# A hybrid decoder step on one core: one-hot rows of the gate table by matrix products and ACT, and the trunk's GpSimd work moved to DVE and ACT

## The chip, the core and the metric

The kernel runs on one core of one Trainium2 chip. A core has a matrix engine (PE, with its weight loads shown apart as PEld), a vector engine (DVE), a scalar engine (ACT), GpSimd (POOL) and SyncE (SP), which here issues nearly all DMAs. Each engine takes its instructions in order. The metric is device time in microseconds of one execution, all DMAs included.

## The reference

One layer is computed for 1024 prompt tokens and 64 sample tokens, D = 1024, in float32 accuracy. The change touches the following parts; the rest (conv and gated recurrence, caches) stays as it is.

```python
z = _rmsnorm(x) @ w_in              # lru_x | lru_gate | q | k | v | gates
p = softmax(scores, sink)           # sliding window attention, 16 heads
hres = x + merged @ w_out
# PEER: per token 8 heads pick 16 of 128*128 experts
qr = (xn @ w_query); s = einsum('nhpd,hpkd->nhpk', qr, sub_keys)
s_top, i_top = lax.top_k(s, 16)
cand_idx = i_top[0] * 128 + i_top[1]        # 16 x 16 pairs of a head
best, pos = lax.top_k(cand, 16)
idx = take_along_axis(cand_idx, pos)        # 128 experts of a token
g = softmax(best)                           # their weights
act = gelu(x . expert_u[idx]) * g ; y = hres + act @ expert_v[idx]
```

## The kernel before

The tokens are worked off in three blocks (block 0: 256 prompt and 64 sample tokens, blocks 1 and 2: 384 prompt tokens each). For each block the *trunk* runs: query, key and value products, attention, the gate and attention branch (L291), the recurrence `lru`, its gate branch (L307), `w_out` (L326), the second norm (`norm_T`, L239 transposes), and `retrieve`, the 16 products with `peer_w_query` and the top 16 of each half (L732 to L739). Every product is done in three passes in fp32r: a weight tile of 128x1024 is loaded (`wraw`), ACT rounds it to `whi` (L148), POOL computes the remainder `wlo` (L149), and `mm3` (L168 to L170) sums hi*hi, hi*lo and lo*hi. Three buffers each of `wraw`, `whi` and `wlo` let weights run ahead.

While the trunk of block 1 runs, the *background* of block 0 is dealt out in small steps by `bg` between trunk steps, and while that of block 2 runs, the background of block 1. It has two parts. `choose` finds a head's 16 best of 50 candidates and fetches their expert numbers by a comparison (L786, DVE), a multiply (L788, POOL) and a sum (L789, DVE). `build_g` then makes the gate table, for each token a 128x128 matrix with the softmax weights at (expert // 128, expert % 128), as the product of two one-hot matrices. It takes tokens by four, a *group*: 176 groups for the 704 tokens of blocks 0 and 1, 8 groups to a *chunk*. A group is two comparisons and two multiplies on DVE and one multiply on POOL of 128x512 bf16 (the weight comes in three bf16 parts), 12 bf16 matmuls into one PSUM tile and one ACT copy into `sg` (L899); a full `sg` (2 MB, one buffer) is stored in `g_d` (L901).

Then `dense` (from 1915 us) multiplies all 128 tiles of 128 experts with those 704 tokens, weighted by the gate table; the 384 tokens of block 2 gather their experts row by row on POOL's queue instead. In that phase the low parts of weights are POOL's too (`ul`, `vl`).

The order on each engine is written out by a scheduler that plays the program through a model of the engines before it runs: instructions are placed when that model has their inputs ready, and PSUM and SBUF buffers of one tag are handed out in the order of the program text. Transposes, the query scores and the gate table share the tag `tr` with three PSUM tiles. The DMAs stand on SP's queue in the order so found, and one that waits holds up those behind it.

Of the kernel before, what the change touches and what calls it, by code (L numbers as in the profile page):

```python
# [63 lines left out]


# [4 lines left out]
class Kern:  # L70
    def __init__(self, ctx, tc, i, o):
        self.ctx, self.tc, self.nc, self.i, self.o = ctx, tc, tc.nc, i, o
        nc = self.nc
# [112 lines left out]
    def load_c(self, src, c0):  # L186

        nc, sp = self.nc, self.sp
        hi = sp.tile([P, KD, P], F32R, tag="whi", name="whi", bufs=NW)
        lo = sp.tile([P, KD, P], F32R, tag="wlo", name="wlo", bufs=NW)  # L190
        raw = sp.tile([P, KD, P], F32, tag="wraw", name="wraw", bufs=NR)
        nc.sync.dma_start(raw, src.rearrange("(k p) c -> p k c", p=P)[:, :, c0:c0 + P])
        self.split(hi, lo, raw, nc.gpsimd)
        return hi, lo

    def load_n(self, src, c0):
# [3 lines left out]
        for h in range(2):  # L200
# [4 lines left out]
            self.split(hi, lo, raw, nc.gpsimd)  # L205
# [161 lines left out]
    def attention(self, bi, xh, xl, ah, al, raw, bg):  # L367
# [46 lines left out]
        def scores(t, j, qT):  # L414
# [28 lines left out]
            nc.gpsimd.tensor_tensor(sb[:, :, 0:S], sb[:, :, 0:S], z4.unsqueeze(2).to_broadcast([P, 4, S]), op=ALU.mult)  # L443
# [378 lines left out]
    def slots_T(self, ft, r, n0):  # L822

        nc = self.nc
        pt = self.tr((P, 3, P))
        for x in range(3):
            nc.tensor.transpose(pt[:, x, 0:r], ft[0:r, x], self.ident[0:r, 0:r])
        sl = self.xp.tile([P, 3, P], F32, tag="sl", name="sl", bufs=1)
        nc.scalar.copy(sl[:, :, 0:r], pt[:, :, 0:r])
        nc.sync.dma_start(self.sT_d[:, :, n0:n0 + r], sl[:, :, 0:r])  # L830
# [39 lines left out]
    def build_g(self, bi):  # L870

        nc, sp = self.nc, self.sp
        p0, p1, smp, nP, n, tiles = self.geom(bi)
        for ch in range(ROW0[bi] // CH, (ROW0[bi] + n) // CH):
            sg = sp.tile([P, AT], F32, tag="at", name="sg", bufs=1)[:, 0:P * CH].rearrange("p (i n) -> p i n", i=P)
            sT = sp.tile([P, 3, CH], F32, tag="sT", name="sT", bufs=1)
            nc.sync.dma_start(sT, self.sT_d[:, :, ch * CH:(ch + 1) * CH])

            s16 = sp.tile([P, 5, CH], BF16, tag="s16", name="s16", bufs=1)
            nc.scalar.copy(s16[:, 0:3], sT)  # L880
            for x in (2, 3):
                nc.vector.tensor_tensor(sT[:, 2], sT[:, 2], s16[:, x], op=ALU.subtract)
                nc.vector.tensor_copy(s16[:, x + 1], sT[:, 2])
            for t4 in range(CH // 4):
                n0 = t4 * 4
                col = lambda x: s16[:, x, n0:n0 + 4].unsqueeze(1).to_broadcast([P, P, 4])
                oij = self.sp.tile([P, 4, P, 4], BF16, tag=self.otag, name="oij", bufs=N4 if self.otag == "s4" else 6)
                oj, wh, wm, wl = (oij[:, x] for x in range(4))
# [4 lines left out]
                nc.vector.tensor_tensor(wh, wh, col(2), op=ALU.mult)
                pt = self.tr()
                for x in range(4):
                    nc.tensor.matmul(pt[:, x, :], oj[:, :, x], wh[:, :, x], start=True, stop=False)
                    nc.tensor.matmul(pt[:, x, :], oj[:, :, x], wm[:, :, x], start=False, stop=False)
                    nc.tensor.matmul(pt[:, x, :], oj[:, :, x], wl[:, :, x], start=False, stop=True)
                nc.scalar.copy(sg[:, :, t4 * 4:t4 * 4 + 4], pt.rearrange("p x i -> p i x"))  # L899
                if t4 == CH // 4 - 1:  # L900
                    nc.sync.dma_start(self.g_d[ch], sg)  # L901
                yield

# [197 lines left out]
```

## Time and profile before

| | us |
|---|---|
| median of 3 runs | 4001.42 (3998.14 to 4010.92) |
| profiled execution, its own time | 3999.96 |
| its span | 3998.0 |
| PE busy / PEld / DVE / ACT / POOL | 3641.4 / 3477.6 / 3151.0 / 1290.8 / 2407.2 |
| block 0 | about 0 to 525 |
| block 1 with the background of block 0 | about 525 to 1245 |
| block 2 with the background of block 1 | about 1245 to 1915 |
| dense phase | 1915 to 3998 |

Busy time counts an engine as busy while at least one of its instructions runs; a PE instruction's end is modelled, so its busy share is read beside others of the same kind rather than as a distance from the peak. In a row of groups, the mean is that of one instruction from its start to its end; where instructions of an engine overlap a little, their starts stand closer than the mean. "Idle before" is the time in which the engine had nothing to run, with what ended it.

### The profile page before, as it was taken

The numbers are of one execution on the slowest core, as the hardware profiler recorded it, in microseconds if no ns is written. First come the engines' busy times: TensorE is split into PE (matmuls) and PEld (weight loads), VectorE is DVE, ScalarE is ACT, GpSimd is POOL, SyncE is SP. The second block draws the span as 40 slices with busy tenths as digits, with TensorE's granted clock in tenths as the row PEclk, the third lists the DMA queues.
The fourth block names the chain that finished last, engine by engine and source line by source line (L and its number), as shares of the span: only waits on it lengthen the run. The fifth ranks groups of instructions, "written<-read, shape, count | busy, mean of one in ns | idle before, by whom it ended". The sixth has DMA issues, their size and how long they took to land. (4 is left out here: it accounts for less than half of the span.)

```text
span 3998.0 us, 60600 instructions
## 1 busy us (share of the span) xinstructions
PE 3641.4 (91%) x22734; PEld 3477.6 (87%) x22734; DVE 3151.0 (79%) x6798; ACT 1290.8 (32%) x2346; POOL 2407.2 (60%) x1560
## 2 busy tenths in 40 slices
PE   7988998778897878998899999999999999999998
PEld 6778978668895777888799999999999999999998
DVE  6365787999899988998987777777777777777773
ACT  4454353443333435333222222222222222222221
POOL 3444546565554664764576677767766767676651
PEclk8989999889997988999899999999999999999999
DMA  5334523234441133444359898999989899899972
GB/s 148 100 111 149 154 72 90 79 101 145 171 139 56 58 94 108 138 173 162 125 204 308 292 318 303 321 323 316 322 295 311 306 319 316 309 317 310 319 259 80
DMA packets 505654, 821.75 MB, mean 206 GB/s; under 512 B 34220, under 2 KB 360812, under 8 KB 502000
## 3 DMA queue, kind: packets, MB, share of 16 engines
q1 hardware_dynamic: 394768, 415.18, 32.5%
q0 software_dynamic: 110592, 402.70, 28.2%
q8 instruction: 178, 2.92, 0.3%
q14 instruction: 116, 0.95, 0.1%
HBM read 753.25 MB, written 66.50 MB: 205 GB/s over the span
## 5 line engine op out<-in xcount | busy, mean ns | idle before, releaser
L149 POOL TENSOR_TENSOR wlo<-wraw,whi 128x1024 fp32r<-128x1024 f32 x252 | 639.3, 2544 | 513.7 <-ACT whi L148 476.0
L168 PE MATMUL ou<-ah,vh 128*128 128x352 f32 x2048 | 663.4, 327 | 40.6 <-ACT ah L148 23.3
L168 PE MATMUL sc<-dx,uh 128*128 128x352 f32 x2048 | 664.6, 325 | 16.2 <-ACT uh L148 9.0
L169 PE MATMUL ou<-al,vh 128*128 128x352 f32 x2048 | 660.1, 325 | 5.3 <-DVE al L149 5.0
L170 PE MATMUL sc<-dx,ul 128*128 128x352 f32 x2048 | 662.0, 323 | 1.0 <-POOL ul L149 1.0
L169 PE MATMUL sc<-dx,uh 128*128 128x352 f32 x2048 | 662.5, 324 | 0.0
L170 PE MATMUL ou<-ah,vl 128*128 128x352 f32 x2048 | 659.0, 324 | 0.0
L859 DVE SCALAR_TENSOR_TENSOR acc<-row,hv,acc 128x1024 f32<-128x1024 f32 x384 | 493.1, 1284 | 157.3 <-DMA row<-in_expert_v,iA 151.6
L847 DVE SCALAR_TENSOR_TENSOR row<-row,xt 128x1024 f32<-128x1024 f32 x384 | 465.5, 1217 | 174.3 <-DMA row<-in_expert_u,iA 165.0
L857 POOL DMA_INDIRECT row<-in_expert_v,iA x384 | 362.2, 943 | 267.8 <-DVE acc L859 192.6
L845 POOL DMA_INDIRECT row<-in_expert_u,iA x384 | 362.4, 944 | 264.4 <-DVE row L847 187.4
L168 PEld LDWEIGHTS ou<-ah,vh 128*128 128x128 f32 x2048 | 385.0, 189 | 55.7 <-ACT ah L148 29.7
L168 PEld LDWEIGHTS sc<-dx,uh 128*128 128x128 f32 x2048 | 386.9, 189 | 20.0 <-DVE al L149 9.8
L148 ACT CAST whi<-wraw 128x1024 fp32r<-128x1024 f32 x252 | 263.9, 1049 | 429.6 <-PE mm L169 167.6
L169 PEld LDWEIGHTS ou<-al,vh 128*128 128x128 f32 x2048 | 387.0, 189 | 7.8 <-DVE al L149 7.8
L170 PEld LDWEIGHTS sc<-dx,ul 128*128 128x128 f32 x2048 | 386.5, 189 | 1.4 <-POOL ul L149 1.4
L169 PEld LDWEIGHTS sc<-dx,uh 128*128 128x128 f32 x2048 | 387.2, 189 | 0.0
L170 PEld LDWEIGHTS ou<-ah,vl 128*128 128x128 f32 x2048 | 386.8, 189 | 0.0
L970 DVE TENSOR_TENSOR dac<-dac,ou 128x352 f32<-128x352 f32 x672 | 339.3, 514 | 59.9 <-PE ou L170 58.0
L149 POOL TENSOR_TENSOR vl<-vn,vh 128x1024 fp32r<-128x1024 f32 x128 | 309.0, 2422 | 65.6 <-ACT vh L148 38.5
L149 POOL TENSOR_TENSOR ul<-un,uh 128x1024 fp32r<-128x1024 f32 x128 | 310.7, 2427 | 45.7 <-ACT uh L148 43.6
L891 POOL TENSOR_TENSOR oij<-oij,s 128x512 bf16<-128x512 bf16 x176 | 225.1, 1290 | 176.9 <-DVE oij L890 132.7
(287 smaller groups left out, 8484.5 us busy)
## 6 DMA issues: line engine op xcount, KB each, us to landing
wraw<-in_w_in SPq DMA_DIRECT2D x132, 512.0 KB
un<-in_expert_uT SPq DMA_DIRECT2D x128, 512.0 KB
vn<-in_expert_v SPq DMA_DIRECT2D x128, 512.0 KB
g_d<-sg SPq DMA_DIRECT2D x22, 2048.0 KB
gt<-g_d SPq DMA_DIRECT2D x64, 704.0 KB
wraw<-in_peer_w_query SPq DMA_DIRECT2D x48, 512.0 KB
wraw<-in_w_branch_attn SPq DMA_DIRECT2D x24, 512.0 KB
wraw<-in_w_branch_lru SPq DMA_DIRECT2D x24, 512.0 KB
```

The source lines that it names most:

```text
L148: nc.scalar.copy(hi, src)
L149: return (lo_eng or nc.vector).tensor_tensor(lo, src, f32(hi), op=ALU.subtract)
L168: nc.tensor.matmul(ps, lh, rh, start=first and j == 0, stop=False)
L169: nc.tensor.matmul(ps, lh, rl, start=False, stop=False)
L170: nc.tensor.matmul(ps, ll, rh, start=False, stop=last and j == n - 1)
L845: nc.gpsimd.indirect_dma_start(out=row, out_offset=None, in_=i["expert_u"], in_offset=bass.IndirectOffsetOnAxis(ap=ia[:, s:s + 1], axis=0))
L847: nc.vector.scalar_tensor_tensor(row, row, 1.0, xt, op0=ALU.mult, op1=ALU.mult, accum_out=hv[:, s:s + 1])
L857: nc.gpsimd.indirect_dma_start(out=row, out_offset=None, in_=i["expert_v"], in_offset=bass.IndirectOffsetOnAxis(ap=ia[:, s:s + 1], axis=0))
L859: nc.vector.scalar_tensor_tensor(acc, row, hv[:, s:s + 1], acc, op0=ALU.mult, op1=ALU.add)
L891: nc.gpsimd.tensor_tensor(wl, wh, col(4), op=ALU.mult)
L970: nc.vector.tensor_tensor(ac[k // 4][:, k % 4, a:b], ac[k // 4][:, k % 4, a:b], ps[:, 0:b - a], op=ALU.add)
```

## The change

Four things change.

1. In `build_g` the one-hot rows no longer come from DVE and POOL. `choose` writes for each slot the row and column number x, its square in two parts and ones as eight bf16 values to DRAM (`ft_d`). `build_g` loads them for 8 tokens at a time as 8x1024 (`fq`), and PE multiplies them with a constant table `fcmp` (8x256), which gives (x - c)^2 for all c of both halves. ACT turns that into relu(1 - d) for the column (L937 of the new kernel, two tokens at once) and relu(w - w*d) for the row, w the softmax weight as ACT's scale and bias (L940, one token each), both in f32. The product of the two is one f32 matmul per token (L912) instead of three bf16 ones. It is issued one group later than its one-hot rows.
2. In `choose` the expert number is found as the least absolute difference of two numbers that carry the candidate's number in steps of 32768, with the expert number added, so POOL's multiply goes.
3. In the attention of the prompt tokens the softmax's scaling, one POOL instruction over four heads, becomes four ACT instructions.
4. `load_c` and `load_n`, the weight loads of the trunk, leave the remainder to DVE. The dense phase keeps POOL.

```diff
@@ setup
...
+        for x in range(2):
+            nc.vector.memset(row[:, 3 * x, x], 128.0)
+            nc.vector.memset(row[:, 3 * x + 1, x], 1.0)
+            nc.vector.tensor_scalar(row[:, 3 * x + 2, x], io, -2.0, None, op0=ALU.mult)
+            nc.vector.tensor_scalar(row[:, 6, x], sq[:, 0], 128.0, None, op0=ALU.mult)
+            nc.vector.tensor_copy(row[:, 7, x], sq[:, 1])
+        nc.sync.dma_start(self.fc_d.rearrange("(o f) x c -> o f x c", o=1), row)
...
+        nc.sync.dma_start(self.fcmp, self.fc_d.rearrange("f x c -> f (x c)"))
@@ load_c, load_n (twice)
         nc.sync.dma_start(raw, src.rearrange("(k p) c -> p k c", p=P)[:, :, c0:c0 + P])
-        self.split(hi, lo, raw, nc.gpsimd)
+        self.split(hi, lo, raw)
@@ attention, scores
-            nc.gpsimd.tensor_tensor(sb[:, :, 0:S], sb[:, :, 0:S], z4.unsqueeze(2).to_broadcast([P, 4, S]), op=ALU.mult)
+            for g in range(4):
+                nc.scalar.activation(sb[:, g, 0:S], sb[:, g, 0:S], AF.Copy, scale=z4[:, g:g + 1])
@@ choose
             bf = xp.tile([P, PH, TOPK], F32, tag="bf", name="bf", bufs=1)
-            nc.vector.tensor_copy(bf[0:r], bi_[0:r])
+            nc.vector.tensor_scalar(bf[0:r], bi_[0:r], float(STEP), None, op0=ALU.mult)
+            nc.vector.tensor_tensor(ce[0:r], ce[0:r], self.iota[0:r].unsqueeze(1).to_broadcast([r, PH, NCAND]), op=ALU.add)
             ev = xp.tile([P, PH, TOPK], F32, tag="ev", name="ev", bufs=1)
             for h in range(PH):
                 eq = xp.tile([P, TOPK, NCAND], F32, tag="eq", name="eq", bufs=2)
-                nc.vector.tensor_tensor(eq[0:r], self.iota[0:r].unsqueeze(1).to_broadcast([r, TOPK, NCAND]),
-                                        bf[0:r, h].unsqueeze(2).to_broadcast([r, TOPK, NCAND]), op=ALU.is_equal)
-                nc.gpsimd.tensor_tensor(eq[0:r], eq[0:r], ce[0:r, h].unsqueeze(1).to_broadcast([r, TOPK, NCAND]), op=ALU.mult)
-                nc.vector.tensor_reduce(ev[0:r, h], eq[0:r], axis=AX.X, op=ALU.add)
+                nc.vector.tensor_tensor(eq[0:r], ce[0:r, h].unsqueeze(1).to_broadcast([r, TOPK, NCAND]),
+                                        bf[0:r, h].unsqueeze(2).to_broadcast([r, TOPK, NCAND]), op=ALU.subtract)
+                nc.vector.tensor_reduce(ev[0:r, h], eq[0:r], axis=AX.X, op=ALU.min, apply_absolute_value=True)
                 yield
...
                 e32 = xp.tile([P, NSLOT], I32, tag="bi", name="e32", bufs=1)
-                i12 = xp.tile([P, 2, NSLOT], I32, tag="cd", name="i12", bufs=1)
+                x12 = xp.tile([P, 2, 3, NSLOT], I32, tag="eq", name="x12", bufs=2)
+                fb = xp.tile([P, NF, NSLOT], BF16, tag="eq", name="fb", bufs=2)
                 nc.vector.tensor_copy(e32[0:r], ev[0:r].rearrange("p h s -> p (h s)"))
-                nc.vector.tensor_scalar(i12[0:r, 0], e32[0:r], 7, None, op0=ALU.arith_shift_right)
-                nc.vector.tensor_scalar(i12[0:r, 1], e32[0:r], 127, None, op0=ALU.bitwise_and)
-                nc.vector.tensor_copy(ft[0:r, 0:2], i12[0:r])
-                late.append((ft, r, r0 + c0))
+                nc.vector.tensor_scalar(x12[0:r, 0, 2], e32[0:r], 7, None, op0=ALU.arith_shift_right)
+                nc.vector.tensor_scalar(x12[0:r, 1, 2], e32[0:r], 127, None, op0=ALU.bitwise_and)
+                nc.vector.tensor_tensor(x12[0:r, :, 0], x12[0:r, :, 2], x12[0:r, :, 2], op=ALU.mult)
+                nc.vector.tensor_scalar(x12[0:r, :, 1], x12[0:r, :, 0], 127, None, op0=ALU.bitwise_and)
+                nc.vector.tensor_scalar(x12[0:r, :, 0], x12[0:r, :, 0], 7, None, op0=ALU.arith_shift_right)
+                nc.scalar.copy(fb[0:r, 0:6], x12[0:r].rearrange("p x f s -> p (x f) s"))
+                nc.vector.memset(fb[0:r, 6:8], 1.0)
+                n0 = r0 + c0
+                nc.sync.dma_start(self.ft_d[:, n0:n0 + r, :].rearrange("f n s -> n f s"), fb[0:r])
+                late.append((ft, r, n0))
                 if len(late) > 1:
                     self.slots_T(*late.pop(0))
                 yield
@@ slots_T
...
+        nc.tensor.transpose(pt[:, 0:r], ft[0:r], self.ident[0:r, 0:r])
+        sl = self.xp.tile([P, P], F32, tag="sl", name="sl", bufs=1)
+        nc.scalar.copy(sl[:, 0:r], pt[:, 0:r])
+        nc.sync.dma_start(self.sT_d[:, n0:n0 + r], sl[:, 0:r])
@@ build_g
...
+        late = []
+        def product(ch, t4, sg, oij):
+            pt = self.tr()
+            for x in range(4):
+                nc.tensor.matmul(pt[:, x, :], oij[:, x, 1], oij[:, x, 0], start=True, stop=True)
+            nc.scalar.copy(sg[:, :, t4 * 4:t4 * 4 + 4], pt.rearrange("p x i -> p i x"))
+            if t4 == CH // 4 - 1:
+                nc.sync.dma_start(self.g_d[ch], sg)
...
+            sw = sp.tile([P, 2, CH], F32, tag="sw", name="sw", bufs=2)
+            nc.sync.dma_start(sw[:, 0], self.sT_d[:, ch * CH:(ch + 1) * CH])
+            nc.scalar.activation(sw[:, 1], sw[:, 0], AF.Copy, scale=-1.0)
...
-                nc.vector.tensor_tensor(oj, self.iota4, col(1), op=ALU.is_equal)
...
-                nc.gpsimd.tensor_tensor(wl, wh, col(4), op=ALU.mult)
-                nc.vector.tensor_tensor(wm, wh, col(3), op=ALU.mult)
...
+                if t4 % (CF // 4) == 0:
+                    n0 = ch * CH + t4 * 4
+                    fq = sp.tile([NF, CF, NSLOT], BF16, tag="fq", name="fq", bufs=2)
+                    nc.sync.dma_start(fq, self.ft_d[:, n0:n0 + CF, :])
+                if t4 == 0 and late:
+                    product(*late.pop(0))
+                if t4 == 0:
+                    sg = sp.tile([P, AT], F32, tag="at", name="sg", bufs=1)[:, 0:P * CH].rearrange("p (i n) -> p i n", i=P)
+                oij = self.sp.tile([P, 4, 2, P], F32, tag=self.otag, name="oij", bufs=N4 if self.otag == "s4" else 6)
+                for x2 in range(2):
+                    ps = self.tr((P, 2, 2, P))
+                    for x in range(2):
+                        m = (t4 * 4) % CF + 2 * x2 + x
+                        nc.tensor.matmul(ps[:, x].rearrange("p a c -> p (a c)"), fq[:, m, :], self.fcmp, start=True, stop=True)
+                    nc.scalar.activation(oij[:, 2 * x2:2 * x2 + 2, 1, :], ps[:, :, 1, :], AF.Relu, scale=-1.0, bias=1.0)
+                    for x in range(2):
+                        m = t4 * 4 + 2 * x2 + x
+                        nc.scalar.activation(oij[:, 2 * x2 + x, 0, :], ps[:, x, 0, :], AF.Relu, scale=sw[:, 1, m:m + 1], bias=sw[:, 0, m:m + 1])
+                if late:
+                    product(*late.pop(0))
+                late.append((ch, t4, sg, oij))
+        for u in late:
+            product(*u)
```

What the scheduler makes of it is shown at three places, as each kernel's rows in the order of its engine. The first is PE at the end of `w_out` in block 2; `oij` are the one-hot rows, `fq` and `fcmp` the new factors, `xn` the input of the second norm's transposes. Before:

```order
L170 MATMUL mm_17667<-whi_17609,gl_17252 128x256
L896 LDWEIGHTS oij_17473
L896 MATMUL tr_17479<-oij_17473 128x128
...
L898 MATMUL tr_17781<-oij_17775 128x128
L239 MATMUL tr_17817<-ident_60,xn_17798 128x128 x4
```

Five groups stand between the last product of `w_out` and the last of the second norm's transposes. Now:

```order
L194 MATMUL mm_17651<-whi_17593,gl_17235 128x256
L936 LDWEIGHTS fq_15947
L936 MATMUL tr_15975<-fcmp_226,fq_15947 128x256
...
L912 MATMUL tr_15981<-oij_15949 128x128 x4
L936 LDWEIGHTS fq_15987
...
L912 MATMUL tr_17772<-oij_17740 128x128 x4
L263 MATMUL tr_17799<-ident_60,xn_17780 128x128 x4
```

Here some 45 groups stand in a row, with no product of the trunk among them except the other two tiles' transposes near the end. In block 1 `w_out` ends with 29 groups issued instead of 43, and a like run of 20 stands in front of that block's second norm.

The second place is ACT in the same run of block 2; before, there are only the copies:

```order
L899 COPY sg_17202<-tr_17479 128x128x4
L899 COPY sg_17202<-tr_17589 128x128x4
L899 COPY sg_17202<-tr_17699 128x128x4
L148 CAST yh_17716<-tr_17741 128x4x128
```

Now, where one chunk ends in `sg_16145` and the next begins in `sg_16376`:

```order
L913 COPY sg_16145<-tr_16358 128x128x4
L920 ACTIVATE sw_16661<-sw_16661 128x32
L913 COPY sg_16145<-tr_16369 128x128x4
L937 ACTIVATE oij_16377<-tr_16378 128x2x128
L940 ACTIVATE oij_16377<-tr_16378,sw_16364 128x128 x2
...
L937 ACTIVATE oij_16477<-tr_16484 128x2x128
L940 ACTIVATE oij_16477<-tr_16484,sw_16364 128x128 x2
L913 COPY sg_16376<-tr_16469 128x128x4
L913 COPY sg_16376<-tr_16490 128x128x4
```

A group is seven instructions now: two of L937, four of L940 and the copy, which stands behind the one-hot rows of the next group. At the turn of a chunk the one-hot rows of three groups (`oij_16377`, `oij_16456`, `oij_16477`) stand between the old chunk's last copy and the new one's first.

The third place is DVE in the gate branch of the recurrence in block 2 (`th` and `mg` are the trunk's own work). Before:

```order
L892 TENSOR_TENSOR oij<-oij,s_15812 128x512 x3
L307 SCALAR_TENSOR_TENSOR th<-th,mm 128x384
L892 TENSOR_TENSOR oij<-oij,s_15812 128x512 x5
L883 CAST s_15812<-sT 128x32
L308 TENSOR_TENSOR mg<-mg,th 128x384
L307 SCALAR_TENSOR_TENSOR th<-th,mm 128x384
L308 TENSOR_TENSOR mg<-mg,th 128x384
L893 TENSOR_TENSOR oij<-oij,s_15812 128x512 x8
```

Now:

```order
L331 SCALAR_TENSOR_TENSOR th<-th,mm 128x384
L173 TENSOR_TENSOR wlo<-wraw,whi 128x1024
L332 TENSOR_TENSOR mg<-mg,th 128x384
L173 TENSOR_TENSOR wlo<-wraw,whi 128x1024
L331 SCALAR_TENSOR_TENSOR th<-th,mm 128x384
L332 TENSOR_TENSOR mg<-mg,th 128x384
L173 TENSOR_TENSOR wlo<-wraw,whi 128x1024 x2
```

The multiplies of the gate table are gone from this queue, and the weights' low parts stand between the trunk's own instructions.

## Rows read from the trace of the kernel before

**Rows 1.** Stretches: us, busy us of each engine, clock granted, DMA share, GB/s

```profile
core 0: us, PE busy (x) PEld busy (x) DVE busy (x) ACT busy (x) POOL busy (x), PEclk, DMA share, GB/s
25.00:525.00 500.00, 446.75 (x3052) 412.27 (x3051) 306.64 (x983) 235.96 (x491) 227.36 (x96) 0.92 0.42 126
525.00:1027.00 502.00, 422.08 (x2541) 378.25 (x2539) 444.99 (x928) 219.75 (x427) 298.19 (x147) 0.93 0.32 101
1027.00:1234.00 207.00, 180.62 (x1282) 173.86 (x1282) 187.50 (x621) 72.93 (x127) 105.43 (x59) 0.94 0.44 143
1245.00:1816.00 571.00, 477.27 (x2911) 425.75 (x2908) 526.35 (x1015) 229.91 (x447) 346.47 (x190) 0.89 0.33 108
1816.00:1912.00 96.00, 89.10 (x564) 87.71 (x563) 77.60 (x425) 28.65 (x45) 31.12 (x13) 0.96 0.46 146
1100.00:1200.00 100.00, 95.62 (x653) 91.84 (x652) 90.73 (x325) 30.64 (x48) 51.95 (x30) 0.98 0.43 140
1200.00:1300.00 100.00, 75.16 (x400) 59.32 (x399) 97.96 (x365) 38.24 (x97) 41.11 (x20) 0.76 0.19 55
1915.00:2045.00 130.00, 113.26 (x644) 108.75 (x645) 127.63 (x368) 38.20 (x55) 87.73 (x41) 0.93 0.33 106
```

**Rows 2.** What PE waited for in blocks 1, then 2: us, times, longest

```profile
PE mm L643 <- ACT ge L636: 18.2, 3, 12.7
...
PE tr L896 <- DVE oij L893: 41.6, 19, 6.1
```

**Rows 3.** Groups of instructions, trunk: count | busy us, mean ns | idle before

```profile
L149 POOL TENSOR_TENSOR wlo<-wraw,whi 128x1024 fp32r<-128x1024 f32 x252 | 639.3, 2544 | 513.7 <-ACT whi L148 476.0 <-PE mm L168 31.1 <-issue 4.1
...
L893 DVE TENSOR_TENSOR oij<-oij,s 128x512 bf16<-128x512 bf16 x176 | 156.0, 902 | 7.2 <-POOL oij L891 7.1
L892 DVE TENSOR_TENSOR oij<-oij,s 128x512 bf16<-128x512 bf16 x176 | 127.7, 743 | 0.2
L889 DVE TENSOR_TENSOR oij<-iota,s 128x512 bf16<-128x512 bf16 x176 | 114.6, 651 | 27.1 <-PE tr L898 27.0
L890 DVE TENSOR_TENSOR oij<-iota,s 128x512 bf16<-128x512 bf16 x176 | 100.2, 569 | 0.0
```

**Rows 4.** Timeline, DVE, a one-hot multiply and a comparison: start us, us

```profile
889.50 1.26 DVE L893 TENSOR_TENSOR oij<-oij,s 128x512 bf16<-128x512 bf16 x1
...
891.01 0.41 DVE L890 TENSOR_TENSOR oij<-iota,s 128x512 bf16<-128x512 bf16 x1
```

**Rows 5.** Groups, trunk: rows that price the added DVE and ACT instructions

```profile
L232 DVE SCALAR_TENSOR_TENSOR xn<-hr,nsy,gb 128x1024 f32<-128x1024 f32 x8 | 10.2, 1280 | 0.1
L362 ACT COPY qn<-mm 128x256 f32<-128x256 f32 x26 | 9.7, 372 | 22.4 <-PE mm L170 22.2
L729 ACT COPY qr<-mm 128x384 f32<-128x384 f32 x32 | 15.2, 474 | 22.1 <-PE mm L170 12.5 <-PE tr L732 9.6
L647 ACT ACTIVATE T<-mm,hb 128x384 f32<-128x384 f32 x16 | 9.3, 580 | 1.7 <-PE mm L643 1.0 <-DVE ll L149 0.7
L443 POOL TENSOR_TENSOR sb<-sb,sm 128x1024 f32<-128x1024 f32 x28 | 55.1, 1970 | 93.9 <-DVE sm L442 59.6 <-DVE sm L437 19.0 <-ACT qT L480 5.3
```

**Rows 6.** Timeline, ACT: three gate-table copies back to back, then a single one

```profile
1742.23 1.55 ACT L899 COPY sg<-tr 128x512 f32<-128x512 f32 x3
...
1747.53 0.59 ACT L899 COPY sg<-tr 128x512 f32<-128x512 f32 x1 [0.83 <-PE tr L898]
```

**Rows 7.** Weight loads of the gate table, group over the trunk

```profile
L896 PEld LDWEIGHTS <-oij 128*128 128x128 bf16 x704 | 82.7, 118 | 71.0 <-DVE oij L893 61.3 <-issue 5.9 <-DVE oij L890 0.5
```

**Rows 8.** Timeline, PE: an f32 product of 128x128 between trunk matmuls

```profile
1862.16 0.38 PE L732 MATMUL tr<-skT,qr 128*128 128x128 f32 x2
...
1862.55 0.34 PE L170 MATMUL mm<-yh,wlo 128*128 128x384 f32 x1
```

**Rows 9.** Timeline: a chunk of the gate table is stored, next copy

```profile
886.77 0.34 SPq L901 DMA_DIRECT2D g_d<-sg  x1
...
894.34 1.19 ACT L899 COPY sg<-tr 128x512 f32<-128x512 f32 x2 [6.07 <-DMA g_d<-sg]
```

More of the change, by code (lines that the diff above doesn't have):

```diff
@@ L38 @@
 NCAND = len(PAIRS)
+STEP = 32768
 SLOPES = [float(np.float32(2.0) ** np.float32(-8.0 * (h + 1) / NH)) for h in range(NH)]
@@ L63 @@
 CH = 32
+NF = 8
+CF = 8
 def f32(ap):
@@ L81, in __init__ @@
         self.kcar_d = self.dr.tile([P, NKV, P], F32, name="kcar_d")
-        self.sT_d = self.dr.tile([P, 3, ND], F32, name="sT_d")
+        self.sT_d = self.dr.tile([P, ND], F32, name="sT_d")
+        self.ft_d = self.dr.tile([NF, ND, NSLOT], BF16, name="ft_d")
+        self.fc_d = self.dr.tile([NF, 2, P], BF16, name="fc_d")
         self.xn2h_d = self.dr.tile([P, KD, ND], F32, name="xn2h_d")
@@ L91, in setup @@
         nc.sync.dma_start(iota, i["c_iota"])
-        nc.vector.tensor_copy(self.iota, iota[:, 0:NCAND])
-        self.iota4 = c.tile([P, P, 4], BF16, name="iota4")
-        nc.vector.tensor_copy(self.iota4, iota.unsqueeze(2).to_broadcast([P, P, 4]))
+        nc.vector.tensor_scalar(self.iota, iota[:, 0:NCAND], float(STEP), None, op0=ALU.mult)
+        row = self.sp.tile([1, NF, 2, P], BF16, tag="s4", name="row", bufs=N4)
+        sq = self.s1([1, 2, P], "sq")
+        si = self.s1([1, 2, P], "si").bitcast(I32)
+        io = iota[0:1, :]
+        nc.vector.memset(row, 0.0)
+        nc.vector.tensor_tensor(si[:, 0], io, io, op=ALU.mult)
+        nc.vector.tensor_scalar(si[:, 1], si[:, 0], 127, None, op0=ALU.bitwise_and)
+        nc.vector.tensor_scalar(si[:, 0], si[:, 0], 7, None, op0=ALU.arith_shift_right)
+        nc.vector.tensor_copy(sq, si)
+        for x in range(2):
[5 more added lines that the diff above has]
+        nc.sync.dma_start(self.fc_d.rearrange("(o f) x c -> o f x c", o=1), row)
+        self.fcmp = c.tile([NF, 2 * P], BF16, name="fcmp")
+        nc.sync.dma_start(self.fcmp, self.fc_d.rearrange("f x c -> f (x c)"))
         self.distP = c.tile([P, 2 * P], F32, name="distP")
@@ L204, in load_n @@
             self.wdma = nc.sync.dma_start(raw, src.rearrange("(k p) c -> p k c", p=P)[:, 4 * h:4 * h + 4, c0:c0 + 256])
-            self.split(hi, lo, raw, nc.gpsimd)
+            self.split(hi, lo, raw)
             out.append((hi, lo))
@@ L794, in choose @@
             else:
-                ft = xp.tile([P, 3, NSLOT], F32, tag="ft", name="ft", bufs=2)
-                gv = ft[:, 2].rearrange("p (h s) -> p h s", h=PH)
+                ft = xp.tile([P, NSLOT], F32, tag="ft", name="ft", bufs=2)
+                gv = ft.rearrange("p (h s) -> p h s", h=PH)
             sz = xp.tile([P, PH], F32, tag="sz", name="sz", bufs=1)
@@ L824, in slots_T @@
         nc = self.nc
[L825 to L830, printed above, removed]
+        pt = self.tr((P, P))
+        nc.tensor.transpose(pt[:, 0:r], ft[0:r], self.ident[0:r, 0:r])
+        sl = self.xp.tile([P, P], F32, tag="sl", name="sl", bufs=1)
+        nc.scalar.copy(sl[:, 0:r], pt[:, 0:r])
+        nc.sync.dma_start(self.sT_d[:, n0:n0 + r], sl[:, 0:r])
     def gather_steps(self, gp, gps):
@@ L873, in build_g @@
         p0, p1, smp, nP, n, tiles = self.geom(bi)
-        for ch in range(ROW0[bi] // CH, (ROW0[bi] + n) // CH):
[L875 to L883, printed above, removed]
-            for t4 in range(CH // 4):
[L885 to L888, printed above, removed]
-                nc.vector.tensor_tensor(oj, self.iota4, col(1), op=ALU.is_equal)
-                nc.vector.tensor_tensor(wh, self.iota4, col(0), op=ALU.is_equal)
-                nc.gpsimd.tensor_tensor(wl, wh, col(4), op=ALU.mult)
-                nc.vector.tensor_tensor(wm, wh, col(3), op=ALU.mult)
[L893 to L901, printed above, removed]
```

## The prediction

> **What bounds the kernel.** I read the stretches first, then what PE waited for, then the groups of instructions, then single timelines. The dense phase runs from 1915 us to the end with PE busy almost throughout, and the change edits only its first 130 us, so the question is the trunk. In block 0, which has no background, PE is busy 446.75 of 500 us (89.3%) with DVE at 61% [rows 1]. Up to the end of `w_out`, blocks 1 and 2 have PE at 84.1% (422.08 of 502) and 83.6% (477.27 of 571), while DVE stands at 89% and 92% [rows 1]. There DVE is the fullest engine, and the longest list of PE's waits in block 2 is for the gate table's one-hot rows: 41.6 us in 19 waits [rows 2]. So the profile says: in blocks 1 and 2 DVE is late, and PE, with a little over a sixth of its time idle, is what would fill up.
>
> **What leaves and what comes, by engine.**
> DVE loses four instructions per group: 156.0 + 127.7 + 114.6 + 100.2 = 498.5 us busy [rows 3]. It gains 252 low parts of 128x1024. The trace has none on DVE; the nearest is a 128x1024 instruction with two SBUF inputs at 1.28 us [rows 5]; the bounds are that and POOL's own 2.54 us [rows 3]. I take 1.28, so 252 x 1.28 = 323 us, two thirds of it (215 us) in blocks 1 and 2. DVE in those two blocks falls by about 280 us, to some 70%.
> POOL leaves the trunk. That matters to DVE twice, because the same 512-element instruction takes 0.41 us at 891.01 and 1.26 us at 889.50 [rows 4], the long one while POOL's multiply runs, so the work that stays on DVE gets shorter too. I put no number on that; it is cover for the 323 us.
> [...]
> ACT gains, per group, two instructions of 256 columns out of PSUM and four of 128 columns with ACT's scale and bias from SBUF. A 256-column copy out of PSUM takes 0.372 us and one of 384 takes 0.474, so 0.80 ns a column [rows 5]; 128 columns then cost 0.27 plain, and 0.376 reckoned down from the 384-column instruction with a bias (0.580) [rows 5]. I take 0.34, nearer the second. With the copy (0.59) a group is 2 x 0.372 + 4 x 0.34 + 0.59 = 2.69 us. Copies back to back start 0.48 us apart (three end after 1.55) [rows 6], about 0.1 us less than one lasts; seven instructions then take 1.95 us of the engine.
> [...]
> The softmax scaling is 4 instructions for one of POOL (1.97 us [rows 5]), 24 times in blocks 1 and 2; at about 0.4 us each ACT gets 38 us. ACT in those blocks had 220 + 73 + 230 + 29 = 552 us [rows 1]; 176 x 1.47 (a group without its copy) and 38 make it 850 of 1390 us, 61%. It is no bound on the average.
> PE: a group was 12 matmuls of about 0.118 us, the pace of their weight loads [rows 7], 1.42 us. Now four bf16 ones of 256 columns, at 0.12, and four f32 products; one such product pushes the next trunk matmul back from 0.17 to 0.39 us over two starts (1862.16 to 1862.55, less the 0.17 of the one between), 0.22 us [rows 8]. 4 x 0.12 + 4 x 0.22 = 1.36 us. Nothing gained.
> At nothing I cost: the setup (about 20 small DVE instructions and two DMAs, covered by the first weight loads; up to 3 us if not), the added DVE work in `choose` (under 2 us per tile of tokens, nine tiles, on an engine that has just been relieved), and the 88 small loads of `fq`. These stand on SP between the weight loads; each waits until PE has used the buffer before last, and the next weights wait behind it. Three weight buffers of about 3.9 us of PE work each cover that; uncovered, it would be some 2 us each in the runs below, 20 us.
>
> **The sum.** Up to the end of `w_out`, blocks 1 and 2 take 502 + 571 = 1073 us with PE busy 899 [rows 1]. By the order, 54 fewer groups are issued there (29 and 51 instead of 43 and 91), 77 us of PE less, and 80 groups are 0.06 shorter: 817 us. What share will PE reach? 89.3% is block 0's, 95.6% the best stretch with much background (1100 to 1200) [rows 1]; I take 92%. 817 / 0.92 = 888: minus 185 us.
> Behind `w_out` those groups come back. In block 2 some 45 stand alone on PE, with ACT the slower partner: 1.95 us per group plus the turn of a chunk. From the issue of the store to the next copy 7.6 us pass (886.77 to 894.34) [rows 9]; ACT fills 3 x 1.47 = 4.4 of them with the next one-hot rows, 3.2 are lost per 8 groups. So 2.4 us a group against PE's 1.36. Block 2: 45 x 2.4 = 108, and the rest of PE's work (89 - 5 x 1.42 = 82 at its own 93%) 88, 196 instead of 96: plus 100. Block 1: 20 groups x 2.4 = 48, the rest 181 - 37 x 1.42 + 31 x 1.36 = 171 at 91% 187, 235 instead of 207: plus 28.
> Block 0 gets its weights sooner (1.28 instead of 2.54 us), but hardly waited for them: minus 8 (0 to 20). The start of the dense phase, PE idle 17 of 130 us behind `choose` [rows 1], loses its POOL multiplies: minus 6.
> -185 + 100 + 28 - 8 - 6 = -71. The profiled execution took 3999.96 us, 1.5 below the median of the runs, so the forecast is 3929 us.
>
> **Rivals.**
> *DVE's relief is worth more.* PE reaches 95.6% (817 / 0.956 = 855, minus 218), and the turn of a chunk hides (2.0 us a group, 26 us less): -218 + 102 - 14 = -130, 3870 us. For it: DVE work shortens beside an idle POOL. Against: block 0 with a half-empty DVE had only 89.3%.
> *No change.* PE's idle time is chains through ACT and the in-order queues (18.2 us in 3 waits of one gate matmul for ACT's gelu [rows 2]), and its share stays near 84 to 86%: 817 / 0.84 = 973 or 950, so 4014 to 3991 us.
> *Slower: a group's chain through ACT doesn't overlap.* Place: the two runs, 65 groups. If PE's comparison, six ACT instructions, product and copy go one after another (0.5 + 1.5 + 0.9 + 0.5 and some 0.15 us for each of four hand-overs), a group takes 4.0 us, 65 x 1.6 = 104 us more: 4033 us. It decides from 3.5 us a group (71 / 65 = 1.1 above 2.4). The three PSUM tiles of `tr` and the one `sg` speak for it, the lag of one group and the order on ACT against. A clock at the lower level would push the same way: 1200 to 1300, with PE at 75%, was granted 0.76 of full speed [rows 1].
>
> **Chances.** Forecast (3895 to 3978) 0.45, better (below 3895) 0.22, no change 0.14, slower 0.19. Runs of this kernel are told from no change at about 0.3%, 12 us; most of the third case lies within it: faster 0.69, same 0.12, slower 0.19. Range 3850 to 4025 us: the better rival's middle and nearly the slower one's, leaving about 0.1 on either side.
>
> **What would show it.** Right: no POOL work before 1750 us, 128x1024 low parts on DVE at 1.2 to 1.3 us, PE at 90% or more before `w_out`, two runs of gate-table products with starts 2.4 us apart, dense phase as long as before. Wrong: products 3.5 us apart or more, PE waiting for `wlo` behind DVE's chains, weight casts on ACT held up by one-hot rows, or PE's share at 84% with an idle DVE.

## The result: 0.5% slower, and the profile after

The changed kernel takes 4021.9 us (median of 12 runs) against 3999.2, a ratio of 1.0051 with a 95% interval of 1.0034 to 1.0068. Its profiled execution took 4013.6 us, span 4011.8. The forecast was 3929 and faster. The stretches of the new trunk follow (columns as in [rows 1]); in block 1 and then in block 2 they end at the last product of `w_out`, at the first and at the last scores of `retrieve`:

```profile
518.00:937.00 419.00, 388.00 (x2161) 327.46 (x2161) 270.40 (x729) 274.63 (x608) 0.00 (x0) 0.94 0.33 103
937.00:1065.00 128.00, 112.58 (x651) 90.92 (x650) 32.29 (x95) 102.41 (x264) 0.00 (x0) 0.81 0.40 141
1065.00:1225.00 160.00, 137.93 (x864) 117.74 (x862) 95.56 (x443) 87.12 (x199) 0.00 (x0) 0.93 0.35 111
1225.00:1696.00 471.00, 432.84 (x2436) 356.20 (x2437) 273.72 (x732) 325.75 (x765) 0.00 (x0) 0.92 0.34 109
1696.00:1853.00 157.00, 144.13 (x638) 111.31 (x637) 15.06 (x39) 126.26 (x334) 0.00 (x0) 0.60 0.32 122
1853.00:1928.00 75.00, 69.42 (x417) 67.53 (x415) 72.81 (x380) 17.15 (x25) 0.00 (x0) 0.96 0.29 85
```

The kernel before by the same marks, the stretch behind `w_out` in one piece (the ends of `w_out` taken in [rows 1], 1027 and 1816, are 3 and 7 us late):

```profile
522.00:1024.00 502.00, 422.40 (x2546) 378.78 (x2545) 444.07 (x936) 221.38 (x429) 295.90 (x147) 0.93 0.32 100
1024.00:1232.00 208.00, 183.31 (x1305) 176.33 (x1304) 188.50 (x624) 72.54 (x129) 105.73 (x59) 0.94 0.44 145
1232.00:1809.00 577.00, 482.50 (x2929) 429.62 (x2930) 532.35 (x1083) 229.91 (x448) 344.75 (x189) 0.88 0.32 107
1809.00:1911.00 102.00, 89.10 (x564) 87.71 (x563) 83.64 (x425) 32.33 (x51) 37.16 (x16) 0.93 0.46 147
```

So blocks 1 and 2 take 890 us up to the end of `w_out` (1079 before: minus 189) and 520 behind it (310 before: plus 210); block 0 gives 4 and the dense phase 3. That sums to plus 14, the difference of the spans; the medians differ by 23. In the fifth row of the new trunk PE is busy 144 of 157 us, and the granted clock is 0.60.

The groups that answer to [rows 3, 5, 7]:

```profile
L173 DVE TENSOR_TENSOR wlo<-wraw,whi 128x1024 fp32r<-128x1024 f32 x252 | 306.9, 1218 | 211.5 <-ACT whi L172 208.2 <-PE tr L936 1.8 <-PE tr L481 0.6
L912 PE MATMUL tr<-oij 128*128 128x128 f32 x1408 | 244.5, 330 | 14.7 <-ACT oij L940 10.8 <-ACT sg L913 2.5 <-DVE yl L173 0.8
L936 PE MATMUL tr<-fcmp,fq 8*128 8x256 bf16 x704 | 145.7, 309 | 15.9 <-ACT oij L940 9.6 <-ACT sg L913 4.3 <-DVE yl L173 1.1
```

A group now has twelve PE instructions again: four comparisons, and eight for the four f32 products. Together they are busy 390 us, 2.2 a group. What they cost hangs on the clock. PE busy and PEld busy of L936, then of L912, first from 800 to 937 us between trunk products, then in the run alone on PE:

```profile
800.00:937.00 137.00, 20.07 (x105) 5.72 (x104) 1.00 0.45 153
800.00:937.00 137.00, 28.48 (x213) 26.99 (x214) 1.00 0.45 153
1720.00:1840.00 120.00, 36.59 (x148) 14.99 (x148) 0.54 0.21 82
1720.00:1840.00 120.00, 76.31 (x311) 66.71 (x312) 0.54 0.21 82
```

At full speed (1.00 granted) a comparison has 0.19 and a product instruction 0.134 us of busy time, 1.83 a group, some of it beside trunk products (from one start to the next it is 0.16 and 0.115, 1.55 a group); in the run, at 0.54 of full speed, mostly at the lower level of 0.50 (so granted from 1760 to 1780 us), both have 0.25, 2.95 a group. A comparison between trunk products also costs its neighbours:

```profile
860.49 0.34 PE L193 MATMUL mm<-ll,whi 128*128 128x384 f32 x1
860.76 0.39 PE L936 MATMUL tr<-fcmp,fq 8*128 8x256 bf16 x2
861.07 0.45 PE L194 MATMUL mm<-lh,wlo 128*128 128x384 f32 x1
861.36 0.34 PE L192 MATMUL mm<-lh,whi 128*128 128x384 f32 x1
```

From start to start the product before it lasts 0.27 and the one behind it 0.29 us, where two trunk products in a row stand 0.17 apart. In blocks 1 and 2, at full clock, the records have 87 and 105 such cases with means of 0.27 and 0.28, 20 us in all.

One period of the run (PE and ACT, some rows left out):

```profile
1703.23 1.03 PE L936 MATMUL tr<-fcmp,fq 8*128 8x256 bf16 x4
1703.33 0.59 ACT L913 COPY sg<-tr 128x512 f32<-128x512 f32 x1 [0.21 <-PE tr L912]
...
1704.19 2.08 PE L912 MATMUL tr<-oij 128*128 128x128 f32 x8
...
1706.19 1.03 PE L936 MATMUL tr<-fcmp,fq 8*128 8x256 bf16 x4
1706.30 0.58 ACT L913 COPY sg<-tr 128x512 f32<-128x512 f32 x1 [0.38 <-PE tr L912]
```

The copies start 2.97 us apart and wait for PE: 0.96 from the first comparison to the first product, 2.00 from there to the next comparison. In block 1, while the clock was still full (1.00 granted from 937 to 945 us), they start 2.37 to 2.42 apart and PE waits for ACT:

```profile
938.85 1.16 PE L912 MATMUL tr<-oij 128*128 128x128 f32 x8 [0.78 <-ACT sg L913]
...
941.27 1.16 PE L912 MATMUL tr<-oij 128*128 128x128 f32 x8
```

### The profile page after: what moved, and what is told of

Read it like the earlier page. It is cut to its first block, busy times and chain, and to the rows that moved or that the text cites. A ratio compares the mean times of both kernels' runs of the same rounds, so it can differ in the third digit from the quotient of the medians.

```text
span 4011.8 us, 60645 instructions
## 1 busy us (share of the span) xinstructions
PE 3752.4 (94%) x22722; PEld 3481.2 (87%) x22722; DVE 2694.6 (67%) x6299; ACT 1690.0 (42%) x3537; POOL 1339.6 (33%) x1028
## 5 line engine op out<-in xcount | busy, mean ns | idle before, releaser
L890 POOL DMA_INDIRECT row<-in_expert_v,iA x384 | 361.0, 940 | 268.1 <-DVE acc L892 189.2
L173 DVE TENSOR_TENSOR wlo<-wraw,whi 128x1024 fp32r<-128x1024 f32 x252 | 306.9, 1218 | 211.5 <-ACT whi L172 208.2
L192 PEld LDWEIGHTS sc<-dx,uh 128*128 128x128 f32 x2048 | 386.7, 189 | 24.8 <-DVE al L173 15.9
L172 ACT CAST ah<-sc 128x352 fp32r<-128x352 f32 x256 | 115.6, 452 | 523.2 <-DVE sc L994 523.1
```

What stands on the lines that cost most here:

```text
L172: nc.scalar.copy(hi, src)
L173: return (lo_eng or nc.vector).tensor_tensor(lo, src, f32(hi), op=ALU.subtract)
L192: nc.tensor.matmul(ps, lh, rh, start=first and j == 0, stop=False)
L890: nc.gpsimd.indirect_dma_start(out=row, out_offset=None, in_=i["expert_v"], in_offset=bass.IndirectOffsetOnAxis(ap=ia[:, s:s + 1], axis=0))
```

## The experiments

Kernels are named by what they change. Ratios are against the kernel before, with 95% intervals; a difference between two changed kernels is that of their ratios, times 4000 us.

**Is it the clock in the run?** Only here PE gets more to do; nothing reads the result:

```diff
+NFILL = 6
...
+            if ch > 16 or (ch == 16 and t4 > 3):
...
+                    for x in range(NFILL):
+                        nc.tensor.matmul(pf[:, 0:256], self.fil[:, 0:P], self.fil, start=True, stop=True)
```

> The changed kernel, with six bf16 products of 128x256 that nobody reads behind each of the 44 groups that stand alone on PE in block 2; the order is otherwise the same. Theory A (PE at the lower clock sets the pace of that run: 2.97 us a group at 0.55 granted, where ACT would need 2.4): the extra work raises the granted clock of the run above 0.9, PE needs 1.65 + 0.65 us a group, ACT paces at 2.4, the run is 44 x 0.6 = 27 us shorter, 3995 us. Rival B (the chain through ACT and the hand-overs set 2.97 whatever the clock) and rival C (PE's price is what it is, the clock does not come back): the extra products cost 6 x 0.21 = 1.3 us a group, 56 us more, 4078 us; under B with a risen clock the pace stays near 3.0, 4020 us.

4013.2 us, 1.0024 (1.0010 to 1.0039). The run without and then with the added work, and one period of copies with it:

```profile
1700.00:1840.00 140.00, 129.01 (x548) 97.59 (x548) 7.34 (x24) 117.74 (x319) 0.00 (x0) 0.55 0.30 113
1700.00:1840.00 140.00, 124.54 (x814) 93.81 (x813) 3.86 (x6) 110.58 (x308) 0.00 (x0) 0.84 0.28 109
```

```profile
1750.47 0.67 ACT L921 COPY sg<-tr 128x512 f32<-128x512 f32 x1
...
1752.85 0.73 ACT L921 COPY sg<-tr 128x512 f32<-128x512 f32 x1
```

The granted clock rises from 0.55 to 0.84, and within a chunk the copies stand 2.38 us apart, at ACT's pace, as theory A said. Yet the run did not shorten: from the last product of `w_out` to the first scores it takes 159 us, 157 in the changed kernel, where 27 less were expected. The first copies of two chunks stand 24.3 us apart (four chunks in 97.3), 24.8 in the changed kernel. There the turn of a chunk hid behind slow PE (1.0 above 8 x 2.97); now it shows, 5.1 above 8 x 2.4. A turn and the chunk behind it:

```profile
1736.50:1745.00 8.50, 6.53 (x31) 4.73 (x31) 0.00 (x0) 6.34 (x19) 0.00 (x0) 0.63 0.53 220
1746.00:1758.00 12.00, 11.65 (x93) 9.03 (x91) 0.00 (x0) 11.82 (x35) 0.00 (x0) 1.00 0.01 4
```

In the turn, with PE busy 6.53 of 8.50 us, the granted clock falls again, to 0.63, and the added products stand in it too. So theory A has the pace right and the time wrong. The 11 us of the ratios are hardly clear of the noise, since the intervals overlap and both profiled spans are 4011.8 us. What a full clock without added work would give stays open.

**Other places for the groups.** Four kernels: background steps dealt out later; earlier; the product's PSUM tile taken from attention's banks; the earlier steps and that tile. The edits of all stand in one fence, with my remarks behind #:

```diff
-PG1 = (5, 5, 4, 5, 2, 2, 0, 0)
-PG2 = (6, 6, 5, 1, 2, 4, 2, 2)
+PG1 = (5, 5, 4, 2, 0, 4, 0, 0)   # later; earlier: (6, 6, 5, 1, 2, 2, 4, 4)
+PG2 = (6, 6, 3, 0, 0, 4, 2, 2)   #        earlier: (6, 6, 5, 1, 2, 4, 4, 4)
-            pt = self.tr()       # product's tile
+            pt = self.pp.tile([P, 4, P], F32, tag="po", name="tg", bufs=2)
```

> The changed kernel with fewer background steps dealt out at the gate branch, w_out and the second norm and more in retrieve (PG1 5,5,4,2,0,4,0,0; PG2 6,6,3,0,0,4,2,2): by the order 16 groups of block 1 and 20 of block 2 move from the runs in front of the second norm to places between the products of retrieve; what is issued up to the end of w_out stays the same. Theory A (runs alone cost 3.06 us a group because the clock falls; between trunk products at full clock a group costs PE 1.55): 36 x 1.5 = 54 us less, 3968 us. Rival C (a group costs PE 2.1 to 3 us anywhere): 0 to 35 us less, 3987 to 4022 us. Rival D (DVE, at 97% in retrieve, cannot take groups beside it): retrieve grows by as much as the runs shrink, 4022 us.

Later: 4040.8 us, 1.0088 (1.0056 to 1.0120). The runs shrink by 53 and 65 us, `retrieve` grows by 63 and 81. That is rival D's outcome, but not its reason: in block 2's `retrieve` (1805 to 1961 us) DVE is busy only 75 of 156 us. Waits there (total, times, longest):

```profile
DVE v L759 <- PE tr L757: 51.7, 7, 17.2
PEld tr L757 <- DVE s L762: 24.4, 28, 1.5
```

Scores and groups share the three `tr` tiles in the order of the text, so DVE's search waits for scores that stand behind groups.

> The changed kernel with the PSUM tile of the gate table's product taken from the two banks of attention's weighted sum instead of the three shared by transposes, scores and comparisons. By the order 160 groups instead of 131.5 are issued by the end of w_out of block 2, 37 instead of 29 in block 1. Theory A: some 36 groups leave the runs for places between trunk products, 36 x 1.5 = 54 us less, 3968 us. Rival C (2.1 us a group anywhere): 35 us less, 3987 us. Rival E (PE's share ahead of w_out cannot rise above 92%, because each group brings its waits along): 36 x (3.06 - 1.55/0.92 - 0.5) = 31 us less, 3990 us.

Tile alone: 3947.5 us, 0.9873 (0.9841 to 0.9905), 71 us off the changed kernel; A was nearest, and its 54 still too small.

> The changed kernel with the background's steps dealt out from attention on (PG1 6,6,5,1,2,2,4,4; PG2 6,6,5,1,2,4,4,4), so that choose runs in attention and the groups follow earlier: by the order all 80 groups of block 1 and 89.5 of 96 of block 2 are issued by the end of w_out; no run of groups alone is left in block 1, one of 6 in block 2. Theory A (a group between trunk products at full clock costs PE 1.55 us, at a share of 92% 1.7; alone at the lower clock 3.06): block 1 saves 139 us behind w_out and pays 51 x 1.7 = 87 ahead of it, block 2 saves 116 and pays 38 x 1.7 = 65: 103 us less, 3919 us. Rival C (2.1 us a group wherever it stands): 68 us less, 3954 us. Rival E (choose and groups in attention lengthen its chains through DVE and ACT): 3960 to 3990 us.

Earlier: 3971.4 us, 0.9907 (0.9878 to 0.9937): rival E.

> The same steps, and the product's PSUM tile from attention's two banks as well; no group is left behind w_out in either block. Theory A: 111 us less than the changed kernel, 3911 us. Rival C: 3949 us, no better than the tile alone (3947.5). Rival E: slower than the tile alone, because the product's tile now stands in the way of attention's weighted sums, 3960 to 3990 us.

Both: 3927.6 us, 0.9798 (0.9759 to 0.9837), between A and C; no run is left.

**The product's price.** One-hot rows in bf16:

```diff
-                oij = self.sp.tile([P, 4, 2, P], F32, tag=self.otag, ...
+                oij = self.sp.tile([P, 4, 2, P], BF16, tag=self.otag, ...
```

> The changed kernel with one-hot rows and weights in bf16 (the softmax weight in the gate table is rounded to bf16), so that the product is one bf16 pass instead of an f32 one; the places of the groups are the same to within 3. Theory A: in the run PE's part falls below ACT's 2.38 us, but the turn of a chunk (5 us per 8 groups) shows in its place, 3.0 us a group, nothing gained there; between trunk products each product saves PE 4 x 0.12 us, 100 groups x 0.48 / 0.92 = 52 us less at most: 3970 to 4000 us. Rival C (the f32 product costs 1.39 us a group wherever it stands, the mean of its rows): 176 x 0.9 = 158 us less, 3865 us.

3958.9 us, 0.9898 (0.9865 to 0.9931). 61 us less, nearer A than C: PE's time for groups falls by 137 us, its idle time grows by 56. But A's "nothing gained there" is wrong. The run of block 2 takes 132 us instead of 157, with as many groups (44) and at the same granted clock. A stretch of it, and the third copies of two chunks:

```profile
1700.00:1800.00 100.00, 72.31 (x346) 40.86 (x346) 5.37 (x7) 89.30 (x249) 0.00 (x0) 0.55 0.30 119
```

```profile
1734.67 0.63 ACT L913 COPY sg<-tr 128x512 f32<-128x512 f32 x1
...
1755.12 0.63 ACT L913 COPY sg<-tr 128x512 f32<-128x512 f32 x1
```

A chunk takes 20.4 us, 1.4 above 8 x 2.38, so 2.55 a group. It was thus PE's price for the f32 product in the run (eight instructions of 0.245 us at 0.54 granted) that held the changed kernel's run at 3.1 us a group; neither ACT nor the turn, by itself, is that slow.

**Part 4, undone and alone.** One argument in two lines (as for part 4 alone; undone, the other way round):

```diff
-        self.split(hi, lo, raw, nc.gpsimd)
+        self.split(hi, lo, raw)
```

> The changed kernel with the trunk's low parts back on POOL (part 4 undone); the places of the groups stay the same to within 2. If DVE's relief comes from the gate table alone, POOL (2.5 us each, three buffers ahead) hides them and the time stays at 4022 within 12 us. If the move of the low parts carries part of the gain of 195 us ahead of w_out, because POOL's work lengthens DVE's and weights come late, it is 30 to 60 us slower, 4052 to 4082 us.

Undone in the changed kernel: 4054.8 us, 1.0145 (1.0115 to 1.0175), 38 us slower than the changed kernel.

> The kernel before with part 4 alone: the trunk's low parts on DVE, all else as it was, the one-hot rows still on DVE and POOL. If busy time simply adds, DVE gets 252 x 1.22 us, 215 us of it in blocks 1 and 2 where it was 89 and 92% busy: 120 to 200 us slower, 4120 to 4200 us. If DVE's instructions were long because POOL worked beside them, and POOL's 640 us are gone, it is 0 to 40 us slower, 4000 to 4040 us.

Alone: 3881.6 us, 0.9699 (0.9660 to 0.9739), better than both expectations. Its DVE does 325 us of low parts more, and its total is lower than before (3151.0):

```profile
PE 3594.4 (93%) x22734; PEld 3441.2 (89%) x22734; DVE 3084.5 (80%) x7050; ACT 1295.3 (33%) x2347; POOL 1796.4 (46%) x1308
L149 DVE TENSOR_TENSOR wlo<-wraw,whi 128x1024 fp32r<-128x1024 f32 x252 | 324.8, 1290 | 72.5 <-ACT whi L148 71.8
L893 DVE TENSOR_TENSOR oij<-oij,s 128x512 bf16<-128x512 bf16 x176 | 103.3, 603 | 6.3 <-POOL oij L891 6.2
L889 DVE TENSOR_TENSOR oij<-iota,s 128x512 bf16<-128x512 bf16 x176 | 85.0, 483 | 21.3 <-PE tr L898 21.1
```

The multiply of L893 fell from 902 ns [rows 3] to 603, the comparison of L889 from 651 to 483.

> The kernel before with part 4, and POOL repeats each of the 252 subtractions behind DVE, into the raw weight tile, whose value nobody needs any more: nobody waits for POOL's result but the next load into that buffer. Theory F (the low parts on POOL cost the trunk because DVE's instructions last longer beside POOL's): DVE's other instructions lengthen again, the one-hot multiplies of L893 from 0.60 to about 0.9 us, and 80 to 120 us of the gain are lost, 3960 to 4000 us. Rival G (what part 4 saves is the wait for low parts that came late from POOL): the low parts come from DVE as early as in part 4 alone, 3882 us within 15.

4185.6 us, 1.0462 (1.0443 to 1.0482), 305 us above part 4 alone and far outside both expectations. The same DVE instructions lengthen again (L899 is the multiply of L893), but the size also has another cause, since weights came later:

```profile
L149 DVE TENSOR_TENSOR wlo<-wraw,whi 128x1024 fp32r<-128x1024 f32 x252 | 388.0, 1542 | 45.0 <-ACT whi L148 44.8
L899 DVE TENSOR_TENSOR oij<-oij,s 128x512 bf16<-128x512 bf16 x176 | 131.4, 764 | 7.8 <-POOL oij L897 7.8
SPq L196 <- POOL wraw L153: 768.1, 129, 17.4
```

So this run can't tell F from G, that part 4 saves the wait for late low parts. The trace of the kernel before speaks against G: of 211 us that PE waited in blocks 1 and 2, 140 were for DVE (97 with part 4 alone), and for POOL's low parts only:

```profile
PE mm L170 <- POOL wlo L149: 4.8, 7, 2.2
```

POOL's last multiply was taken away as well, which holds nothing longer. First the kernel it is compared with, then that one:

> The kernel before with parts 2, 3 and 4: only the gate table stays as it was, its one-hot rows on DVE and POOL. If the gate table alone turns the gain of part 4 into the loss (theory H), this stays near part 4 alone, 3850 to 3900 us; POOL loses another 55 + 110 us of work beside DVE, which speaks for the lower half. If the softmax scaling on ACT or the new search in choose carries part of the loss, it is 3900 us or more.

3870.2 us, 0.9667 (0.9649 to 0.9686): theory H, without a gain that could be told from part 4 alone.

```diff
-                nc.gpsimd.tensor_tensor(wl, wh, col(4), op=ALU.mult)
+                nc.vector.tensor_tensor(wl, wh, col(4), op=ALU.mult)
```

> Parts 2, 3 and 4, and the third one-hot multiply of the old gate table (POOL, 1.3 to 1.4 us each) on DVE too, so that POOL has nothing left in the trunk. No buffer is held longer and nothing is waited for that was not before. Theory F (POOL's work lengthens DVE's): the three multiplies of DVE take 0.40 to 0.45 us each instead of 0.50 to 0.59, the comparisons as well, so that DVE's busy time changes by 176 x 0.45 = 79 us less some 60, and the time stays within 15 us of 3870. If busy time simply adds up, DVE (some 90% busy ahead of w_out) is 79 us longer and the time 30 to 80 us more, 3900 to 3950 us.

3873.6 us, 0.9689 (0.9661 to 0.9717): theory F. The first and last of DVE's five instructions, and the page's totals (DVE was 3030.3 with four):

```profile
PE 3609.9 (93%) x22734; PEld 3453.4 (89%) x22734; DVE 2977.0 (77%) x7235; ACT 1343.2 (35%) x2473; POOL 1343.0 (35%) x1028
L891 DVE TENSOR_TENSOR oij<-iota,s 128x512 bf16<-128x512 bf16 x176 | 74.0, 420 | 33.2 <-PE tr L900 32.9
L895 DVE TENSOR_TENSOR oij<-oij,s 128x512 bf16<-128x512 bf16 x176 | 67.3, 418 | 0.1
```

With POOL idle five instructions of a group take 0.42 us each, 352 us in all; before, four took 498 [rows 3]. DVE got one instruction more per group and was less busy. The time is the same, so by then DVE no longer held the kernel.

> Part 4 alone, with the background's steps dealt out from attention on (PG1 6,6,5,1,2,2,4,4; PG2 6,6,5,1,2,4,4,4): by the order no group is left behind w_out, where part 4 alone leaves 47 and 21. If groups behind w_out cost more than groups ahead of it here too (PE is busy 81% of the 140 us behind w_out in block 2), 20 to 60 us less, 3820 to 3860 us. If attention's chains through DVE lengthen by the same, 3880 us or more.

3896.9 us, 0.9744 (0.9711 to 0.9777): no gain. The stretches up to `w_out` lengthen by 173 us, those behind it lose 160.

**Part 3.** In the changed kernel PE waits 15.8 us for scaled scores in block 2:

```profile
PE tr L481 <- ACT sb L468: 15.8, 3, 8.4
```

> The changed kernel with the softmax scaling back on POOL (part 3 undone); the places of the groups stay the same to within 4. Theory A (the loss sits in PE's time for the groups): 0 to 15 us either way, 4007 to 4037 us. Rival I (the scaling stands in ACT's queue among the one-hot rows and holds up attention's transposes, 15.8 us of PE's waits in block 2): 15 to 40 us less, 3980 to 4007 us.

4000.2 us, 1.0003 (0.9987 to 1.0018), 19 us less than with part 3: rival I.

> The kernel before with parts 2 and 4: gate table and softmax scaling as they were. Part 3 cost 19 us in the changed kernel, where ACT also makes one-hot rows. If it is the scaling's four instructions on ACT that cost (rival I), this is 10 to 20 us faster than parts 2, 3 and 4, 3850 to 3860 us; if it is only their meeting with the one-hot rows there, the two are the same within 8, 3862 to 3878 us.

3858.8 us, 0.9648 (0.9626 to 0.9671), the fastest of all kernels here. Whether part 3 costs anything beside the old gate table stays open: the interval overlaps that of parts 2, 3 and 4.

## Why the prediction was wrong

PE's time up to the end of `retrieve` in block 2, added up over all its matmul records (each to its end or the next start) and split by the granted clock:

| us | old table, part 1 absent: before | part 4 | parts 2, 3, 4 | all four | all four, own tile, earlier |
|---|---|---|---|---|---|
| end of the trunk | 1911 | 1802 | 1788 | 1928 | 1848 |
| groups at full clock | 205 | 216 | 217 | 196 | 276 |
| groups at the lower level | 41 | 30 | 28 | 158 | 19 |
| other matmuls | 1383 | 1344 | 1363 | 1393 | 1400 |
| idle | 282 | 213 | 180 | 182 | 154 |

The first step, "DVE is late", was right as a reading of the rows and wrong as a cause. DVE was full because POOL worked beside it. I saw the same instruction take 0.41 and 1.26 us [rows 4], called it cover and "put no number on that"; it was the largest term of the change. Those rows are a comparison and a multiply; the comparison of L890 alone took 0.41 us at 891.01, with POOL idle, and 1.25 at 891.68, where POOL's multiply ran from 891.60 to 892.66. Part 4 alone is worth 120 us although DVE gets 325 us of work: the multiply of L893 took 902 ns before, 603 with part 4 alone and 418 with POOL idle in the trunk. I gave the shorter DVE work to a rival instead of the sum.

The forecast of 888 us up to `w_out` met 890, with PE's busy time at 821 (817 forecast) and its share at 92.6 and 91.9% (92). So the size was right and its owner wrong: with the old gate table and parts 2, 3 and 4 the same stretches take 907 us, though 114 groups and not 80 are issued in them. Once the low parts are off POOL, taking one-hot rows off DVE leaves PE's idle time as it is (180 and 182): its waits for DVE fall from 97 to 68 us, those for ACT rise from 72 to 101.

The step that failed is the second: the groups "come back" at plus 128, measured plus 210 (block 1 plus 80 for 28, block 2 plus 130 for 100). Its wrong term is PE's price of a group, 1.36 us, by which ACT would set the pace of the runs. From start to start a group takes 1.59 us at full clock (a comparison 0.16 and not 0.12, a product 0.24 and not 0.22). And the clock, which the prediction named beside a rival and gave no price, falls in the runs (0.54 granted from 1720 to 1840 us), where a group takes 2.97.

By the table's records a group instruction takes 0.133 us at full clock and 0.245 at the lower level; 643 instructions x 0.112 are 72 us, two thirds of the 108 by which the new groups exceed the old. That is PE's time, and not all of it is the kernel's: with bf16 products PE's groups lose 137 us and the kernel 61. Of the 30 us missed in block 2 they give back 25 in the run. Where no run is left (last column), the new groups still take 50 us more of PE than the old, and the kernel is 52 us slower than with parts 2, 3 and 4. Of the 140 us between the third and fourth columns, 30 lie in other matmuls; the neighbours of comparisons explain some 20.

The old groups paid nothing for a slow clock: their weight loads, the pace, are as long at 0.77 granted as at 0.99 (by the records of the kernel before an instruction takes 0.116 us at full clock and 0.118 at the lower level). PE busy and PEld busy of the old L898 with parts 2, 3 and 4:

```profile
1663.00:1714.00 51.00, 17.45 (x59) 6.98 (x58) 0.77 0.58 218
1400.00:1600.00 200.00, 56.29 (x190) 21.98 (x190) 0.99 0.46 153
```

6.98 / 58 = 0.120 and 21.98 / 190 = 0.116 us. Two errors of the same sum nearly cancel, by luck: ACT, reckoned at 1.95 us a group, gives 2.38, and a turn, where PE is quick enough, takes 1.4 and not 3.2 us, 2.55 a group for 2.4.

In block 1, 31 groups stand ahead of `retrieve`'s first scores; the prediction priced the 20 of the longest run at 2.4 and the other 11 as if between trunk products. The bf16 products gain nothing there (289 us behind `w_out`, 288 in the changed kernel); the product's own tile gives back 59, with 8 groups fewer. How the 52 us missed divide between the shared tile and the order stays open.

Block 0 (minus 4 for 8) and the dense phase (minus 3 for 6) were right in sign and small. Part 3, costed as 38 us on an ACT that is no bound, costs 19 in the changed kernel. The slower rival was near in time (4033) by another road: the chain of a group does overlap (2.97 us a group in the run, not 4.0); PE itself was slow.

## What to carry over

Before an engine is called full, divide its rows by the shortest duration of the same instruction in a timeline: if it lengthens beside another engine, moving that engine's work onto it can empty it (here DVE's total fell from 3151.0 to 3084.5 us with 325 us of low parts added). Work that moves from a full helper engine to PE is priced at the clock of the place where it lands, and small products left alone on PE landed here at 0.54 of full speed, 2.95 us of busy time a group where it had been 1.83. Test the parts of a change alone: here one argument in two lines held the gain of 3%, and the new gate table spent it.

## What was not expected of the hardware

PE was busy 129 of 140 us in the run of block 2 and the granted clock was 0.55; six more bf16 products of 128x256 per group brought 0.84, and the run took as long. And a 128x512 bf16 instruction of DVE took 0.42 us beside an idle POOL, 0.48 to 0.60 with part 4 alone, where POOL still makes one-hot rows, and 0.57 to 0.90 where it makes the low parts as well.
